# Value products of the samples as ScalarE copies, and the samples' loads issued from Pool's queue

## Chip, cores, metric

One core of one Trainium2 chip runs the whole kernel as one launch. The metric is the device time of one execution in microseconds; lower is better. The core has TensorE (PE in the profile), VectorE (DVE), ScalarE (ACT), GpSimd (POOL) and SyncE (SP). DMAs are issued by an engine's queue and moved by 16 DMA engines that all queues share.

## The reference, cut to what matters

The kernel computes one inference step of a two-layer decoder for a prompt of 1024 tokens and, sharing all weights, for 8 samples of one token each. Both layers have a mixer and a SwiGLU feed-forward part; both mixers hold a cross-attention over 256 memory tokens with 4 heads of 128, and layer 1 also holds a stick-breaking attention. For the samples the keys and values of these attentions are caches in HBM: `cache_mem_k` and `cache_mem_v` per layer and sample, and a paged pool `cache_sb_k`, `cache_sb_v`, of which each sample owns two pages of 128 tokens. So a sample's attention is one query row against 256 keys, and it shares no keys with the other samples.

```python
def mem_attend(q, mk, mv):
    s = jnp.einsum('blhd,bmhd->bhlm', q, mk) * (q.shape[-1] ** -0.5)
    p = jax.nn.softmax(s, axis=-1)
    return jnp.einsum('bhlm,bmhd->blhd', p, mv)

def stick_breaking(q, k, v, bias, q_pos, k_pos):   # per block of queries
    z = jnp.einsum('bqhd,bkhd->bhqk', qi, kf) * scale + bf
    log_keep = jnp.where(mask, jax.nn.log_sigmoid(-z), 0.0)
    tail = lax.cumsum(log_keep, axis=3, reverse=True) - log_keep
    w = jnp.where(mask, jnp.exp(jax.nn.log_sigmoid(z) + tail), 0.0)
    return jnp.einsum('bhqk,bkhd->bqhd', w, vf)
```

## The kernel before, in words

**Tiling.** The prompt is split in two groups of 512 tokens; group 1 also carries the 8 samples as 8 more columns (520). Activations stand with features on the 128 partitions. Every projection (`proj`, L256) is a product in three passes of float32r: weights and activations are split into a high and a low part, and high x high, high x low and low x high are added in PSUM. For it `split_w` (L240) loads weights of 4 x 128 rows by 128 columns from SyncE's queue (L245), casts them on ScalarE (L250) and subtracts on VectorE (L251). Raw weights have 5 buffers and split weights 5. Each projection of 1024 rows needs two such tiles; a down-projection in these parts one.

**Order of the work.** The code is a set of Python generators that are woven together by counts (`weave`), and the tile framework lays out each engine's own instruction sequence when the kernel is built; engines and queues then run in that sequence and wait on semaphores. The samples' work is in three streams, each woven with a part of a feed-forward network of the other group:

- `a1.mem_sample()` (layer 0, memory attention), with `f0.part(2)` and `f0.part(3)`;
- `b1.sb_sample()` (layer 1, stick-breaking over the pages), then
- `b1.mem_sample()` (layer 1, memory attention), both with `f0.part(2)` and `f0.part(3)` of layer 1.

A feed-forward part has gate and up projections first, with `silu` (L274: four ScalarE and two VectorE instructions) and the product L472 behind them, and then the down-projections, whose results VectorE adds up (L401).

**A sample stage.** `sample_scores` (L669) copies the queries (L672), transposes them on TensorE (L677), copies them to SBUF (L679) and writes them to a small HBM tile `qd` (L681). Then for each sample: load its keys, a tile `kt` of 128 partitions x 2 x 512 (512 KB); read its query row back from `qd`, repeated on all 128 partitions (`qb`, 256 KB, L687); multiply (L688); reduce each head's 128 columns (L689). `sample_pv` (L694) loads the sample's values `vt` in the same layout, multiplies each 128-column head block by the weight of that key and head (L700, one VectorE instruction over 128 x 1024), adds the two key halves (L701) and lets TensorE sum over the partitions with a selection matrix (L702), which puts each sample into its own row of one PSUM tile. `mem_loader` loads keys and values with one plain DMA (L717); `page_loader` gathers two pages with two indirect DMAs issued on Pool (L729).

**Buffers.** Key and value tiles come from `C()` (4 buffers of 128 x 1024 float32, also used for the memory's keys and values of the prompt and others), `qb` from `B()` (7 buffers), projections' PSUM from a pool of 2, other PSUM tiles from one of 3.

Of the kernel before, what the change touches and what calls it, by code (L numbers as in the profile page):

```python
# [12 lines left out]
AF = mybir.ActivationFunctionType  # L13
# [4 lines left out]
P = 128  # L18
# [4 lines left out]
def tile_decoder(  # L23
# [6 lines left out]
    nc = tc.nc  # L30
    D = x_prompt.shape[2]
    ND = D // P
    NB = x_sample.shape[0]
    NM = mem_prompt.shape[1]
    H = 4
# [32 lines left out]
    def nm(s):  # L68
        uid[0] += 1
        return f"{s}_{uid[0]}"  # L70
# [4 lines left out]
    def B(dt=F32):  # L75
        return bpool.tile([P, 512], dt, tag="b", name=nm("b"))
# [24 lines left out]
    def C():  # L101
        return cpool.tile([P, 2, 512], F32, tag="c", name=nm("c"))

    def S():
        return smp.tile([P, 512], F32, tag="s", name=nm("s"))

    def small(shape, dt=F32, tag="sm", bufs=None):
        return spool.tile(shape, dt, tag=tag, name=nm(tag), bufs=bufs)
# [39 lines left out]
    for lv in range(7):  # L148
# [3 lines left out]
        src = ones[:, 0:64].rearrange("p (b m) -> p b m", m=m)  # L152
        nc.gpsimd.affine_select(
            mf, src, pattern=[[-2 * m, nb], [0, m]], compare_op=ALU.is_ge, fill=0.0, base=0, channel_multiplier=1
# [115 lines left out]
    def split_to(dst, src):  # L270
        nc.scalar.copy(dst[0], src)  # L271
        nc.vector.tensor_sub(dst[1], src, dst[0].bitcast(F32))  # L272
# [396 lines left out]
    def sample_scores(q, load, sc):  # L669
        qc = small([P, H * NB], tag="ss")  # L670
        for i in range(2):
            nc.vector.tensor_copy(  # L672
                qc[:, i * 2 * NB : (i + 1) * 2 * NB].rearrange("p (h b) -> p h b", h=2), q[i][:, :, G : G + NB]
            )
        pq = S()
        for h in range(H):
            nc.tensor.transpose(pq[:NB, h * P : (h + 1) * P], qc[:, h * NB : (h + 1) * NB], ident)  # L677
        qt = B()
        nc.vector.tensor_copy(qt[:NB, :], pq[:NB, :])  # L679
        qd = tc.dram_tile([NB, 512], F32, name=nm("qd"))  # L680
        nc.sync.dma_start(qd, qt[:NB, :])  # L681
        yield
        scv = sc.rearrange("p (k h b) -> p k h b", k=2, h=H)
        for b in range(NB):
            kt = load(b)
            qb = B()
            nc.sync.dma_start(qb, qd[b].partition_broadcast(P))  # L687
            nc.vector.tensor_mul(kt, kt, qb.unsqueeze(1).to_broadcast([P, 2, 512]))  # L688
            nc.vector.tensor_reduce(  # L689
                scv[:, :, :, b], kt.rearrange("p k (h d) -> p k h d", h=H), axis=AX.X, op=ALU.add  # L690
            )
            yield

    def sample_pv(pT, load, xo, k0):  # L694
        po = S()
        pv4 = pT.rearrange("p (k h b) -> p k h b", k=2, h=H)
        for b in range(NB):
            vt = load(b)
            v4 = vt.rearrange("p k (h d) -> p k h d", h=H)
            nc.vector.tensor_mul(v4, v4, pv4[:, :, :, b].unsqueeze(3).to_broadcast([P, 2, H, P]))  # L700
            nc.vector.tensor_add(vt[:, 0, :], vt[:, 0, :], vt[:, 1, :])  # L701
            nc.tensor.matmul(po[:NB, :], sel[:, b, :], vt[:, 0, :], start=(b == 0), stop=(b == NB - 1))  # L702
            yield
        ot = B()
        nc.vector.tensor_copy(ot[:NB, :], po[:NB, :])
        pr = S()
        for h in range(H):
            nc.tensor.transpose(pr[:, h * NB : (h + 1) * NB], ot[:NB, h * P : (h + 1) * P], ident[:NB, :NB])
        for h in range(H):
            d = xo[k0 + h]  # L710
            split_to((d[:, 0, G : G + NB], d[:, 1, G : G + NB]), pr[:, h * NB : (h + 1) * NB])
        yield

    def mem_loader(src, l):
        def load(b):
            t = C()
            nc.sync.dma_start(t, src[l, b].rearrange("(k p) h d -> p k (h d)", p=P))  # L717
            return t

        return load  # L720
# [16 lines left out]
    def mem_attn_sample(l, qm, xo):  # L737
        HB = H * NB
        sc = small([P, 2 * HB], tag="sc", bufs=2)
        yield from sample_scores(qm, mem_loader(cache_mem_k, l), sc)  # L740
        pr = S()
        for blk in range(2):
            nc.tensor.transpose(pr[:HB, blk * P : (blk + 1) * P], sc[:, blk * HB : (blk + 1) * HB], ident)
        nmx = small([P, 2], tag="nmx")
        nc.vector.tensor_reduce(nmx[:HB, 0:1], pr[:HB, :NM], axis=AX.X, op=ALU.max, negate=True)
        sm = small([P, 2], tag="sme")
        pe = B()
        nc.scalar.activation(pe[:HB, :NM], pr[:HB, :NM], AF.Exp, bias=nmx[:HB, 0:1], accum_out=sm[:HB, 0:1])
        nc.vector.reciprocal(sm[:HB, 0:1], sm[:HB, 0:1])
        nc.vector.tensor_scalar(pe[:HB, :NM], pe[:HB, :NM], sm[:HB, 0:1], None, op0=ALU.mult)  # L750
        pb = S()
        for blk in range(2):
            nc.tensor.transpose(pb[:, blk * HB : (blk + 1) * HB], pe[:HB, blk * P : (blk + 1) * P], ident[:HB, :HB])
        pT = small([P, 2 * HB], tag="ss")
        nc.vector.tensor_copy(pT, pb[:, : 2 * HB])
        yield
        yield from sample_pv(pT, mem_loader(cache_mem_v, l), xo, H)
# [320 lines left out]
    def sb_sample(Qs, xo):  # L1078
        HB = H * NB
        zb = small([P, 2 * HB], tag="sc", bufs=2)  # L1080
        yield from sample_scores(Qs, page_loader(cache_sb_k), zb)
        nc.vector.tensor_add(zb, zb, biass.rearrange("p k h b -> p (k h b)"))
        e = small([P, 2 * HB], tag="ss")
        softplus_sp(zb, e, 2 * HB)
        cu = S()
        nc.tensor.matmul(cu[:, 0:HB], trif, e[:, 0:HB], start=True, stop=False)
        nc.tensor.matmul(cu[:, 0:HB], ones, e[:, HB : 2 * HB], start=False, stop=True)
        nc.tensor.matmul(cu[:, HB : 2 * HB], trif, e[:, HB : 2 * HB], start=True, stop=True)
        nc.vector.tensor_sub(zb, zb, cu[:, : 2 * HB])
        nc.scalar.activation(zb, zb, AF.Exp)  # L1090
        yield
        yield from sample_pv(zb, page_loader(cache_sb_v), xo, 0)
# [133 lines left out]
```

## Time and profile before

| what | value |
|---|---|
| runs shown | median 2563.17 us of 3 (2561.86 to 2564.59) |
| profiled execution | 2560.6 us, span 2558.9 us |
| TensorE, VectorE, ScalarE, GpSimd busy | 2525.4, 1556.9, 1218.0, 48.8 us |
| mean granted TensorE clock | 0.992 |
| SyncE's DMA queue | 454954 packets, 286.92 MB |
| issues concerned: L717, L687, L681 | 32 of 512 KB, 24 of 256 KB, 3 of 16 KB |
| median from issue to landing: L717, L687, L729 | 3.7, 6.1, 3.8 us |

How to read it: busy time of an engine is given with its share of the span and the number of instructions. Line rows name the line, the engine, the operation and the tiles written and read, then how often, the busy time and mean duration, and the idle time of that engine just before with what ended it. In a timeline the columns are start, duration, engine, line, operation, tiles and count, then in brackets the idle time before and its releaser. Matmuls overlap, so a single one's duration is longer than its share of the engine's time.

### The profile page before, as it was taken

The numbers are of one execution on the slowest core, as the hardware profiler recorded it, in microseconds if no ns is written. First come the engines' busy times: TensorE is split into PE (matmuls) and PEld (weight loads), VectorE is DVE, ScalarE is ACT, GpSimd is POOL, SyncE is SP. The second block draws the span as 40 slices with busy tenths as digits, with TensorE's granted clock in tenths as the row PEclk, the third lists the DMA queues.
The fourth block names the chain that finished last, engine by engine and source line by source line (L and its number), as shares of the span: only waits on it lengthen the run. The fifth ranks groups of instructions, "written<-read, shape, count | busy, mean of one in ns | idle before, by whom it ended". The sixth has DMA issues, their size and how long they took to land.

```text
span 2558.9 us, 40442 instructions
## 1 busy us (share of the span) xinstructions
PE 2525.4 (99%) x15649; PEld 2203.6 (86%) x15649; DVE 1556.9 (61%) x2709; ACT 1218.0 (48%) x2290; POOL 48.8 (2%) x59
## 2 busy tenths in 40 slices
PE   8999999999999999999999999999999999999998
PEld 6888898888777888999999989767776798999998
DVE  6666466654765577555544577666677758444445
ACT  6346543343434445555433455566543245443334
POOL 1000000000000000000000000000041000000000
PEclk9999999999999999999999999999999999999999
DMA  6352242233642445322333445322156444333332
GB/s 186 111 158 71 74 149 81 60 111 112 202 144 87 128 154 178 105 81 63 99 92 93 127 151 180 111 87 67 53 180 211 148 125 124 110 88 101 94 92 68
DMA packets 457707, 297.90 MB, mean 116 GB/s; under 512 B 17573, under 2 KB 422642, under 8 KB 457514
## 3 DMA queue, kind: packets, MB, share of 16 engines
q1 hardware_dynamic: 454954, 286.92, 37.2%
q0 software_dynamic: 2560, 8.39, 1.1%
q8 instruction: 123, 2.02, 0.3%
q14 instruction: 70, 0.57, 0.1%
HBM read 265.44 MB, written 29.80 MB: 115 GB/s over the span
## 4 chain that ended last, share of the span: by engine, by line
issue 25%; PE 23%; DVE 1%; POOL 1%; DMA 0%; ACT 0%; DVEq 0%; POOLq 0%
PE mm L264 22%; POOL c L729 1%; PE s L702 0%; DMA c<-in_cache_sb_k,pidx 0%; DVE ws L251 0%; DVE sc L689 0%; DMA b<-qd 0%; DVE t L280 0%; DMA c<-in_cache_sb_v,pidx 0%; PE s L1123 0%; PE ns L291 0%; PE s L438 0%; DVE yT L540 0%; DVE t L283 0%; DVE c L688 0%
## 5 line engine op out<-in xcount | busy, mean ns | idle before, releaser
L264 PE MATMUL mm<-x,ws 128*128 128x260 f32 (+1 forms) x10080 | 1676.2, 324 | 10.7 <-DVE ws L251 4.2
L264 PEld LDWEIGHTS mm<-x,ws 128*128 128x128 f32 x10080 | 1451.1, 189 | 171.7 <-issue 21.5
L251 DVE TENSOR_TENSOR ws<-w,ws 128x512 fp32r<-128x512 f32 (+1 forms) x800 | 522.5, 657 | 533.5 <-ACT ws L250 522.6
L250 ACT CAST ws<-w 128x512 fp32r<-128x512 f32 (+1 forms) x800 | 474.3, 593 | 694.0 <-PE mm L264 624.1
L264 PE MATMUL mm<-m,ws 128*128 128x260 f32 (+1 forms) x3168 | 543.2, 326 | 1.1 <-DVE r L401 0.6
L264 PEld LDWEIGHTS mm<-m,ws 128*128 128x128 f32 x3168 | 453.8, 188 | 59.9 <-issue 15.0
L277 ACT ACTIVATE t<-mm 128x512 f32<-128x512 f32 (+1 forms) x104 | 62.5, 601 | 195.8 <-PE mm L264 195.7
L401 DVE TENSOR_TENSOR r<-r,mm 128x520 f32<-128x520 f32 (+1 forms) x128 | 88.3, 690 | 97.6 <-PE mm L264 96.5
L472 DVE TENSOR_TENSOR t<-t,mm 128x512 f32<-128x512 f32 (+1 forms) x88 | 60.8, 691 | 72.2 <-PE mm L264 72.1
L280 DVE SCALAR_TENSOR_TENSOR t<-mm,t 128x512 f32<-128x512 f32 (+1 forms) x104 | 72.1, 693 | 43.6 <-ACT t L279 43.4
L281 ACT ACTIVATE t<-t 128x512 f32<-128x512 f32 (+1 forms) x104 | 65.9, 634 | 11.8 <-DVE t L280 11.7
L302 DVE TENSOR_TENSOR st<-st,n 128x512 f32<-128x512 f32 (+1 forms) x98 | 67.0, 690 | 6.5 <-ACT n L301 4.6
L279 ACT ACTIVATE t<-t 128x512 f32<-128x512 f32 (+1 forms) x104 | 66.0, 635 | 2.8
L278 ACT ACTIVATE t<-t 128x512 f32<-128x512 f32 (+1 forms) x104 | 66.2, 637 | 0.0
L283 DVE TENSOR_TENSOR t<-t,mm 128x512 f32<-128x512 f32 (+1 forms) x88 | 60.3, 685 | 5.4 <-ACT t L281 4.8
L271 ACT CAST m<-t 128x512 fp32r<-128x512 f32 (+1 forms) x88 | 54.9, 623 | 18.0 <-DVE t L472 11.3
L272 DVE TENSOR_TENSOR m<-t,m 128x512 fp32r<-128x512 f32 (+1 forms) x88 | 61.0, 693 | 3.9 <-ACT m L271 1.9
L729 POOL DMA_INDIRECT c<-in_cache_sb_k,pidx x16 | 22.7, 1416 | 1869.9 <-DVE r L401 1244.1
L890 PEld LDWEIGHTS s<-a,a 128*128 128x128 f32 x448 | 53.4, 192 | 1.2
L890 PE MATMUL s<-a,a 128*128 128x64 f32 x448 | 53.2, 271 | 0.0
L1025 DVE SCALAR_TENSOR_TENSOR b<-b,b 128x512 f32<-128x512 f32 (+3 forms) x48 | 26.8, 558 | 30.6 <-ACT b L1024 30.1
L641 ACT ACTIVATE b<-s,nmx 128x256 f32<-128x256 f32 x64 | 29.7, 469 | 28.2 <-DVE nmx L635 28.2
(291 smaller groups left out, 1960.9 us busy)
## 6 DMA issues: line engine op xcount, KB each, us to landing
w<-in_w_gu SPq DMA_DIRECT2D x352, 256.0 KB, 2.9
w<-in_w_down SPq DMA_DIRECT2D x160, 256.0 KB, 2.7
w<-in_w_in_a SPq DMA_DIRECT2D x80, 256.0 KB, 3.0
w<-in_w_o SPq DMA_DIRECT2D x64, 256.0 KB, 2.8
w<-in_w_mem_kv SPq DMA_DIRECT2D x32, 256.0 KB, 3.0
c<-in_cache_mem_k SPq DMA_DIRECT2D x16, 512.0 KB, 3.7
c<-in_cache_mem_v SPq DMA_DIRECT2D x16, 512.0 KB, 3.7
w<-in_w_kv SPq DMA_DIRECT2D x32, 256.0 KB, 3.0
```

Of the source, the lines that this page charges most:

```text
L250: nc.scalar.copy(ws[:, 0, :n, :], raw[:, :n, :])
L251: nc.vector.tensor_sub(ws[:, 1, :n, :], raw[:, :n, :], ws[:, 0, :n, :].bitcast(F32))
L264: nc.tensor.matmul(ps[:, a, : PW[g]], wt, xt[k][:, xi, o : o + PW[g]], start=(k == 0 and wi == 0), stop=(k == nk - 1 and wi == 2),)
L272: nc.vector.tensor_sub(dst[1], src, dst[0].bitcast(F32))
L277: nc.scalar.activation(av, pv(ps, g), AF.Abs)
L278: nc.scalar.activation(av, av, AF.Exp, scale=-1.0)
L279: nc.scalar.activation(av, av, AF.Ln, bias=1.0)
L280: nc.vector.scalar_tensor_tensor(av, pv(ps, g), 0.0, av, op0=ALU.min, op1=ALU.subtract)
L281: nc.scalar.activation(av, av, AF.Exp)
L302: nc.vector.tensor_add(acc[:, :n], acc[:, :n], t[:, :n])
L401: nc.vector.tensor_add(dst, dst, pv(ps, g))
L890: nc.tensor.matmul(plv[:, hh, c, :], K_[:, hh, cs], rhs, start=True, stop=True)
```

## The change

Two things are edited. In `sample_pv` the one VectorE product per sample becomes eight ScalarE copies, one for each key half and head, each over 128 columns and scaled by the weight column of that half, head and sample; the add of the two halves stays on VectorE and the sum on TensorE. And three kinds of DMA of the sample stages are issued by Pool in place of SyncE: the write of the queries to `qd`, the broadcast reads of `qd`, and the plain loads of memory keys and values. The page gathers were on Pool already.

```diff
@@ sample_scores
         qd = tc.dram_tile([NB, 512], F32, name=nm("qd"))
-        nc.sync.dma_start(qd, qt[:NB, :])
+        nc.gpsimd.dma_start(qd, qt[:NB, :])
...
             kt = load(b)
             qb = B()
-            nc.sync.dma_start(qb, qd[b].partition_broadcast(P))
+            nc.gpsimd.dma_start(qb, qd[b].partition_broadcast(P))
@@ sample_pv
             v4 = vt.rearrange("p k (h d) -> p k h d", h=H)
-            nc.vector.tensor_mul(v4, v4, pv4[:, :, :, b].unsqueeze(3).to_broadcast([P, 2, H, P]))
+            for k in range(2):
+                for h in range(H):
+                    nc.scalar.activation(v4[:, k, h, :], v4[:, k, h, :], AF.Copy, scale=pv4[:, k, h, b : b + 1])
@@ mem_loader
             t = C()
-            nc.sync.dma_start(t, src[l, b].rearrange("(k p) h d -> p k (h d)", p=P))
+            nc.gpsimd.dma_start(t, src[l, b].rearrange("(k p) h d -> p k (h d)", p=P))
```

## The prediction

> **What bounds the kernel now.** I read the page first, for the share of each engine, then the windows by stage around the three sample stages, then the timeline of the worst of them, and last the lines that the change touches.
>
> ```profile
> PE 2525.4 (99%) x15649; PEld 2203.6 (86%) x15649; DVE 1556.9 (61%) x2709; ACT 1218.0 (48%) x2290; POOL 48.8 (2%) x59
> ...
> q0 software_dynamic: 2560, 8.39, 1.1%
> ```
>
> TensorE is busy for 99% of the span, so only its idle stretches and its clock can move. The samples' work stands in three stages: about 647 to 767 us (layer 0, memory attention), 1875 to 1956 (layer 1, stick-breaking over the pages), 1957 to 2034 (layer 1, memory attention). Each has a score part (L688, L689) and a value part (L700 to L702). The windows by stage, in order: score and value of the pages, score and value of layer 1's memory, score and value of layer 0's memory (columns: stretch, its length, then busy time and count of PE, PEld, DVE, ACT, POOL, the granted clock, DMA share, GB/s):
>
> ```profile
> 1885.50:1902.50 17.00, 12.91 (x52) 9.70 (x51) 16.94 (x20) 5.48 (x10) 11.41 (x8) 0.90 0.76 244
> 1926.50:1948.80 22.30, 21.46 (x80) 12.59 (x79) 19.13 (x25) 3.10 (x5) 8.90 (x8) 1.00 0.55 166
> 1963.50:1984.00 20.50, 17.06 (x73) 13.18 (x71) 20.40 (x24) 9.38 (x16) 0.00 (x0) 1.00 0.76 241
> 2011.40:2031.30 19.90, 19.90 (x71) 10.66 (x70) 18.63 (x24) 2.49 (x4) 0.00 (x0) 1.00 0.39 129
> 655.00:684.00 29.00, 27.58 (x120) 22.15 (x119) 28.72 (x35) 12.66 (x21) 0.00 (x0) 1.00 0.90 277
> 721.00:748.00 27.00, 27.00 (x107) 18.33 (x108) 22.81 (x31) 8.79 (x15) 0.00 (x0) 1.00 0.58 175
> ```
>
> In the score parts VectorE has no free time (16.94 of 17.00, 20.40 of 20.50, 28.72 of 29.00) and TensorE idles 4.09, 3.44 and 1.42 us. In the value parts VectorE is busy too, but TensorE idles only 0.84 us in the first and nothing in the others. The timeline of the pages' score part shows how:
>
> ```profile
> 1885.56 1.23 DVE L688 TENSOR_TENSOR c<-c,b 128x1024 f32<-128x1024 f32 x1 [0.63 <-DMA b<-qd]
> ...
> 1899.88 2.49 DVE L251 TENSOR_TENSOR ws<-w,ws 128x512 fp32r<-128x512 f32 x4
> 1899.95 5.50 POOL L729 DMA_INDIRECT c<-in_cache_sb_k,pidx x1 [0.30 <-issue]
> 1900.62 12.30 PEld L264 LDWEIGHTS mm<-x,ws 128*128 128x128 f32 x44 [3.10 <-DVE ws L251]
> 1900.62 23.83 PE L264 MATMUL mm<-x,ws 128*128 128x512 f32 x92 [2.67 <-DVE ws L251]
> ```
>
> The weight splits (L251) queue behind score products, and TensorE waits for them. The wait costs twice: an undisturbed pair of projections, x48, takes 11.05 us (at 655.88), 0.230 each, so 92 would take 21.2 and took 23.83, at a granted clock of 0.71 in 1900 to 1910. After the idle time at 1984 the next 44 took 11.88 in place of 10.1. So 7.5 us of idle time in these two places brought 4.4 us at a low clock: 0.58 us for each us idle.
>
> **The change, part by part.** The rows that price it:
>
> ```profile
> L688 DVE TENSOR_TENSOR c<-c,b x24: 1211/1218/1258, 654.9 to 1986.8; 128x1024 f32<-128x1024 f32 x24
> ...
> L701 DVE TENSOR_TENSOR c<-c x24: 677/683/686, 723.3 to 2028.1; 128x512 f32<-128x512 f32 x24
> ...
> L250 ACT CAST ws<-w 128x128 fp32r<-128x128 f32 x64 | 19.0, 297 | 88.8 <-PE mm L264 81.8 <-issue 5.3 <-ACT b L641 1.5
> ...
> L353 ACT ACTIVATE x<-ns,par 128x512 fp32r<-128x512 f32 x8 | 5.6, 695 | 2.5 <-PE ns L350 2.5
> ```
>
> **Removed from VectorE:** 24 products of L700 at 1.22 us, 29.2 us, all in the value parts. The only TensorE time there to gain is the idle 0.84 us; the score parts' VectorE work (24 x (1.218 + 1.212) = 58.3 us) is untouched. Gain 0.8, bounds 0 and 0.8.
>
> **Added to ScalarE:** 8 copies of 128x128 for each of 24 samples, 192 in all, 64 in each value part. A plain 128x128 cast takes 0.297; a copy with a scale per partition takes 0.695 at 128x512 (L353), and an element costs (0.619 - 0.297)/384 = 0.84 ns between the two sizes of L250, so 0.695 - 0.322 = 0.373 at 128x128. Independent neighbours start closer than they last (L277 at 600.61 lasts 0.60, the next starts 0.49 later). From start to start I bound it by 0.28 and 0.40 and take 0.31, nearer the overlapped row since the eight touch different columns. 64 x 0.31 = 19.8 us. With what ScalarE already does in the three value parts (3.10, 2.49, 8.79) this makes 22.9 in 22.3, 22.3 in 19.9, 28.6 in 27.0: over by 0.6, 2.4 and 1.6, sum 4.6. At 0.28 the sum is 0.5, at 0.40 it is 22. ScalarE thus becomes the engine of the value part. Queued behind the copies there are its weight casts (L250), for which L251 and then TensorE wait; their cover is five split buffers, each half a gate projection, 5 x 2.76 = 14 us of matmuls. The samples' own matmul (L702) stands in TensorE's order with down-projections around it, and 20 of these (4.9 us) still follow the last one at 2033.71. I charge half: 2.3 us, bounds 0 and 22.
> By the Trainium skill (ScalarE: Activation LUTs, What ACT_TABLE_LOAD costs) an activation takes 186 ns and 0.833 ns per element, 93 more for a pointer operand, and neighbours overlap by 93. That gives an estimate of 386 ns lasting and 293 from start to start, so 18.8 us a part and an overrun of 2.0 in place of 4.6; the row's 373 agrees with the first figure, and no row here shows the second.
>
> **Moved from SyncE's queue to Pool's:** 32 loads of memory K and V, 24 query broadcasts, 3 writes of the queries, 59 in all. Their bytes are the same. Buffers set the loads' times: SyncE issued the fifth K load at 660.27, as the first reduction ended, so on Pool they go no earlier. SyncE is rid of 59 issues of 0.3 to 0.46 us and of their waits, but no weight came late for these: it stood still from 1887 to 1900.6 because the splits that free weight buffers were late. I count 0, with 1 us either way.
> The price of a plain load on Pool is not in the trace. Near rows are the gathers: 0.945 us plus 0.30 to the next in quiet time, 1.25, and 8 of them from 1888.79 to 1905.45, 2.08 each, beside a full VectorE (one lasted 5.50). Below, 0.30 as on SyncE. I take 1.25. What is late then is the start of each score part: write, then first broadcast, in sequence. In the third stage the write was issued at 1958.05, the first broadcast at 1959.53, and VectorE, after waiting 2.02 us, began at 1963.51. Two dearer issues add 2 x 0.95 - 0.30 - 0.43, about 1.2, and a gap of 0.3: 1.5 us; at 2.08 each 3.4. In the page stage Pool also has gathers at 1880.35 and 1881.60, just when the query write is wanted (1879.26): 1.5 if the write stands ahead of them, 4.8 behind; I take 3. Sum 1.5 + 1.5 + 3 = 6.0, bounds 0 and 12. VectorE is full right behind each start, so this is backlog for the splits; the buffers ahead soften it. I take 0.6, 3.6 us of TensorE idle time, and 0.58 of that for the clock, 2.1.
>
> **Sum:** -0.8 + 2.3 + 0 + 3.6 + 2.1 = +7.2 us. The profiled execution took 2560.6 us (span 2558.9), 2.6 below the median 2563.2; carried to the median 2570.
>
> **The rivals.**
> **Faster.** The score part's cost is a burst: eight products and reductions ahead of four splits. Broadcasts that arrive one per Pool issue, not seven within 3.8 us as at 1881.27, could let splits pass between them. At stake are 4.09 + 3.44 + 1.42 idle and 4.4 of clock, 13.4 us; half of it gives 2556. For it: the burst is plain in the rows. Against it: VectorE's demand stays. An x48 step of TensorE (11.05) carries 5.4 us of splits and gate work and 2.5 samples at 2.43, 11.5 in all, and an in-order VectorE that waits for a broadcast lets no split pass.
> **Pool feeds too slowly.** If every issue costs the 2.08 us of the full stretch, the eight broadcasts that join the page gathers put its last score up to 16.6 us later. Half of it lost, with its clock, is 8.3 x 1.58 = 13 on top of 7: 2583. For it: the gather of 5.50 us ran while VectorE had two-input work back to back. Against it: a plain load reads no index, and VectorE, once it waits, leaves Pool alone.
> The Trainium skill (SBUF — State Buffer, SBUF: two separate sides) says that VectorE and GpSimd share a port pair, and that descriptors for a DMA issued on Pool can't be written while VectorE holds it, so such loads are better issued from SP. The 5.50 us fits; no run here shows a plain load under it.
> **ScalarE copies at 0.40 us:** overrun 22, half exposed, with clock 17, and 5.7 of late starts: 2586. For it: eight small instructions for one. Against it: the overlap seen in L277.
> **Everything hidden:** later starts are absorbed by the ready splits and ScalarE keeps pace: 2563.
>
> **How the numbers follow.** Forecast 0.43, own range 2563 to 2580; hidden 0.20; faster 0.15; Pool 0.12; ScalarE 0.10. I call within 0.2% (5.1 us) no change, about what a measurement here can tell. Slower: the last two and four fifths of the forecast, 0.57, and a little of the hidden case, 0.59; faster 0.15; the rest, 0.26, is no change. From 2556 to 2588 leaves out the tails of the faster and the ScalarE case.
>
> **What would show it.** Right: VectorE's first L688 of each stage 1.5 to 5 us later against its query copy (L679); ScalarE near 9 tenths in the value parts, its copies 0.3 us apart; TensorE's idle time in the score parts up by some 4 us, waiting for L251, with a clock dip behind it. Wrong: Pool issues at SyncE's price, or TensorE idle less in the score parts (then the faster rival); TensorE waiting at L702 for ScalarE by more than 3 us a part (then the ScalarE rival); VectorE waiting for key loads in mid-part (then Pool).

## The result, and the profile after

The changed kernel took 2566.64 us (median of 22 runs, 2563.1 to 2573.12), the kernel before 2561.7 us on the same chip (22 runs, 2554.05 to 2564.88). The ratio is 1.0025, with a 95% interval from 1.0018 to 1.0032: slower by 4.9 us between the medians and by 6.4 by the ratio, which is not that of the medians; +7.2 was forecast. The profiled execution of the changed kernel has a span of 2565.3 us, 6.4 more than before's, at a mean granted clock of 0.991.

The edit shifts the line numbers: the copies are L702, the add of the halves L703, the sample's matmul L704, the plain loads L719, the page gathers L731.

The page of the kernel after, busy time of each engine, then the queue that Pool feeds (packets, MB, share):

```profile
PE 2527.6 (99%) x15649; PEld 2202.8 (86%) x15649; DVE 1530.4 (60%) x2685; ACT 1273.0 (50%) x2482; POOL 85.1 (3%) x118
...
q0 software_dynamic: 9184, 31.51, 3.8%
```

VectorE works 26.5 us less, ScalarE 55.0 more, GpSimd 36.3 more, and TensorE still works for all but some 38 us of the span. So the few lost microseconds are in short places. The windows by stage of the kernel after, in the order of the prediction's table (score and value of the pages, of layer 1's memory, of layer 0's memory):

```profile
1887.00:1904.00 17.00, 11.35 (x44) 8.32 (x43) 16.44 (x19) 5.27 (x9) 11.52 (x9) 0.87 0.64 223
1927.00:1950.00 23.00, 23.00 (x83) 13.11 (x82) 9.82 (x16) 20.36 (x68) 9.64 (x10) 1.00 0.52 156
1965.00:1998.50 33.50, 27.37 (x107) 21.46 (x107) 28.74 (x34) 12.22 (x22) 7.54 (x12) 0.90 0.67 211
2015.00:2038.50 23.50, 22.58 (x77) 11.31 (x75) 10.10 (x17) 21.92 (x70) 2.86 (x4) 1.00 0.34 104
655.00:684.00 29.00, 27.72 (x121) 22.23 (x120) 28.57 (x35) 12.65 (x21) 5.62 (x8) 1.00 0.86 274
721.00:748.00 27.00, 27.00 (x106) 17.86 (x106) 13.13 (x21) 24.79 (x74) 2.90 (x4) 1.00 0.50 161
```

Read the idle time of TensorE as length less busy time. In the value part of layer 1's memory ScalarE is now all but full (21.92 of 23.50) and VectorE has time to spare (10.10); the same holds for layer 0's (24.79 of 27.00). Layer 0's stage loses next to nothing: TensorE idles 1.28 us in its score part, 1.42 before, and none in its value part, as before. In the third row TensorE idles 6.13 us.

The totals of two single profiles don't locate a loss of 5 us. Some low-clock time between 514 and 644 us, ahead of all samples' work, differs between the profiles of kernels that are alike there, and moved single spans by -6 to +1.7 us. So the start of the n-th projection matmul (L264) was compared between the two traces, n by n: TensorE runs the projections in the same order in all kernels, and the growth of the difference within a stage is what that stage lost. For the kernel after, in us of before's time:

```
15-514   514-644   644-804   804-1672   1672-1954   1954-2004   2004-2041   2041-2540   all
 +0.0      -0.0      +0.2      -0.3       +0.7        +3.5        +1.9        +0.0      +6.3
                  layer 0's memory         pages     score part  value part
                                                     of layer 1's memory
```

Nearly all of it, 5.4 of 6.3 us, is in the last of the three stages. Its start in the kernel after (columns: start, duration, engine, line, operation, tiles and count, then idle time before it and its releaser):

```profile
1939.85 2.45 ACT L702 ACTIVATE c<-c,sc 128x128 f32<-128x128 f32 x8 [0.69 <-DMA c<-in_cache_sb_v,pidx]
...
1949.55 2.68 ACT L250 CAST ws<-w 128x512 fp32r<-128x512 f32 x5
...
1958.22 0.68 DVE L679 COPY b<-s 8x512 f32<-8x512 f32 x1 [0.18 <-PE s L677]
...
1959.20 0.56 POOL L681 DMA_DIRECT2D qd<-b  x1 [6.62 <-DVE b L679]
...
1962.54 3.76 POOL L687 DMA_DIRECT2D b<-qd  x7 [2.78 <-DMA qd<-b]
...
1967.04 2.36 DVE L688 TENSOR_TENSOR c<-c,b 128x1024 f32<-128x1024 f32 x2 [4.69 <-DMA b<-qd]
...
1972.90 14.05 PE L264 MATMUL mm<-x,ws 128*128 128x512 f32 x50 [3.83 <-DVE t L283]
```

and the same place in the kernel before:

```profile
1957.34 0.68 DVE L679 COPY b<-s 8x512 f32<-8x512 f32 x1 [0.19 <-PE s L677]
...
1958.05 0.30 SPq L681 DMA_DIRECT2D qd<-b  x1
...
1959.53 3.30 SPq L687 DMA_DIRECT2D b<-qd  x6
...
1963.51 2.36 DVE L688 TENSOR_TENSOR c<-c,b 128x1024 f32<-128x1024 f32 x2 [2.02 <-DMA b<-qd]
...
1969.38 11.62 PE L264 MATMUL mm<-x,ws 128*128 128x512 f32 x50 [1.15 <-DVE t L283]
```

Count from the query copy (L679). Before: write after 0.71, first broadcast after 2.19, first score product after 6.17 us. After: 0.98, 4.32, 8.82. The product is 2.65 us later, VectorE stands idle for 4.69 in place of 2.02, everything behind it on VectorE is late, and TensorE waits 3.83 in place of 1.15 us for a gate's last product (L283). The next 50 matmuls then take 14.05 in place of 11.62 us. In windows of 6 us the granted clock is 0.94 from 1966, 0.50 from 1972 and 0.99 from 1978 in the kernel after, which makes 6.8 us at half speed; before it is 0.72 from 1984 and full around it, 3.4 us at half speed. So the part pays 2.7 us of idle time and up to 1.7 of clock, and comes out 3.5 later. The wait that grew is the one for the gate's last product; TensorE's other two in this part, for L472 (0.77 us) and for a weight split (L251, 1.53 and 1.54), are as long as before.

Two more things are to be seen. Most of the lateness lies between write and first broadcast, that is, in the landing of 16 KB in HBM (from issue to issue 1.48 us before, 3.34 after). And ahead of it ScalarE runs five weight casts in a row at 1949.55, behind the copies; before, they stand apart, at 1946.10, 1948.88, 1953.68, 1956.47 and 1960.15. The last copies themselves wait for page values, 2.6 us in three waits, and the casts stand behind them in ScalarE's sequence. What the casts do to the DMAs is seen in windows (stretch, length, busy time and count of PE, PEld, DVE, ACT, POOL, clock, DMA share, GB/s), first before:

```profile
1950.00:1953.00 3.00, 3.00 (x12) 1.99 (x11) 1.92 (x4) 0.00 (x0) 0.00 (x0) 1.00 0.86 228
...
1956.00:1959.00 3.00, 3.00 (x19) 2.21 (x18) 2.12 (x5) 1.01 (x4) 0.00 (x0) 1.00 0.47 148
1959.00:1962.00 3.00, 3.00 (x15) 2.49 (x14) 1.02 (x3) 0.79 (x2) 0.00 (x0) 1.00 0.59 165
```

then after:

```profile
1950.00:1953.00 3.00, 3.00 (x11) 1.42 (x10) 3.00 (x6) 2.23 (x5) 1.43 (x2) 1.00 0.27 86
...
1956.00:1959.00 3.00, 3.00 (x19) 2.25 (x18) 1.37 (x2) 0.40 (x1) 0.00 (x0) 1.00 1.13 328
1959.00:1962.00 3.00, 3.00 (x15) 2.49 (x14) 1.53 (x6) 1.41 (x6) 0.56 (x1) 1.00 0.98 232
```

Raw weight buffers come free when they have been cast and split. Held back and then cast in one go, they let the next weights go out in a lump: the DMA share is 0.27 while the buffers are held and 1.13 and 0.98 just when the queries are written and read back, where before it was 0.47 and 0.59.

### The profile page after: what moved, and what is told of

The parts are those of the page before. It is cut to its first block, busy times and chain, and to the rows that moved or that the text cites. A ratio compares the mean times of both kernels' runs of the same rounds, so it can differ in the third digit from the quotient of the medians.

```text
span 2565.3 us, 40650 instructions
## 1 busy us (share of the span) xinstructions
PE 2527.6 (99%) x15649; PEld 2202.8 (86%) x15649; DVE 1530.4 (60%) x2685; ACT 1273.0 (50%) x2482; POOL 85.1 (3%) x118
## 3 DMA queue, kind: packets, MB, share of 16 engines
q8 instruction: 123, 2.02, 0.3%
## 4 chain that ended last, share of the span: by engine, by line
PE 54%; DVE 3%; ACT 1%; issue 1%; DMA 1%; POOL 0%; DVEq 0%; ACTq 0%; SPq 0%; POOLq 0%
PE mm L264 47%; PE s L1063 1%; PE s L1075 1%; PE s L1048 1%; PE s L661 1%; PE s L704 1%; PE s L630 1%; DVE ws L251 0%; DMA b<-qd 0%; PE s L654 0%; PE ns L291 0%; DVE sc L689 0%; DVE c L688 0%; DVE st L302 0%; PE s L1004 0%
## 5 line engine op out<-in xcount | busy, mean ns | idle before, releaser
L264 PE MATMUL mm<-x,ws 128*128 128x260 f32 (+1 forms) x10080 | 1676.7, 324 | 14.2 <-DVE t L283 7.7
L264 PEld LDWEIGHTS mm<-x,ws 128*128 128x128 f32 x10080 | 1451.4, 189 | 176.7 <-issue 23.6
L251 DVE TENSOR_TENSOR ws<-w,ws 128x512 fp32r<-128x512 f32 (+1 forms) x800 | 522.8, 658 | 532.3 <-ACT ws L250 527.3
L264 PE MATMUL mm<-m,ws 128*128 128x260 f32 (+1 forms) x3168 | 544.4, 326 | 1.1 <-DVE r L401 0.6
L264 PEld LDWEIGHTS mm<-m,ws 128*128 128x128 f32 x3168 | 453.4, 188 | 62.9 <-issue 17.5
L472 DVE TENSOR_TENSOR t<-t,mm 128x512 f32<-128x512 f32 (+1 forms) x88 | 60.8, 691 | 71.4 <-PE mm L264 71.2
L283 DVE TENSOR_TENSOR t<-t,mm 128x512 f32<-128x512 f32 (+1 forms) x88 | 60.3, 686 | 5.5 <-ACT t L281 4.8
L731 POOL DMA_INDIRECT c<-in_cache_sb_k,pidx x16 | 22.2, 1387 | 1134.9 <-PE s L630 1127.3
```

Source lines behind the costliest of these rows:

```text
L251: nc.vector.tensor_sub(ws[:, 1, :n, :], raw[:, :n, :], ws[:, 0, :n, :].bitcast(F32))
L264: nc.tensor.matmul(ps[:, a, : PW[g]], wt, xt[k][:, xi, o : o + PW[g]], start=(k == 0 and wi == 0), stop=(k == nk - 1 and wi == 2),)
```

## The experiments

All were timed in five rounds against the kernel before on the same chip; a ratio is to that kernel, with its 95% interval, and a cost in us is worked out from the ratio. The first question was which edit costs: the copies, the queries' two DMAs, the keys and values, or only some of them together. The rivals of the late start were that the copies alone cost all, and that Pool feeds the keys and values too slowly.

### The copies alone

```diff
 (against the change: all loads back on SyncE)
-        nc.gpsimd.dma_start(qd, qt[:NB, :])
+        nc.sync.dma_start(qd, qt[:NB, :])
...
-            nc.gpsimd.dma_start(qb, qd[b].partition_broadcast(P))
+            nc.sync.dma_start(qb, qd[b].partition_broadcast(P))
...
-            nc.gpsimd.dma_start(t, src[l, b].rearrange("(k p) h d -> p k (h d)", p=P))
+            nc.sync.dma_start(t, src[l, b].rearrange("(k p) h d -> p k (h d)", p=P))
```

> Only the ScalarE copies; all sample loads stay on SyncE. Theory A (the loss is the late query broadcast of the last sample stage, 2.7 us of TensorE idle time and 1.7 us of clock, and the copies cost about 1.9 us in the last value part and give back what they gain in the others): +0.5 to +2.0 us against before, with the third stage's first L688 again about 3 us ahead of where the changed kernel has it. Rival B (the copies are the loss): +4 to +6 us. Rival C (the key and value loads on Pool are the loss): 0 to +2 us as in A.

Measured: 2562.41 us, 1.0004 [0.9992, 1.0017]. No difference can be told from this time. By segments the value part of layer 1's memory loses 1.9 us, as in the change, and its score part 0.4.

### The loads alone

```diff
 (against the change: the product back on VectorE)
-            for k in range(2):
-                for h in range(H):
-                    nc.scalar.activation(v4[:, k, h, :], v4[:, k, h, :], AF.Copy, scale=pv4[:, k, h, b : b + 1])
+            nc.vector.tensor_mul(v4, v4, pv4[:, :, :, b].unsqueeze(3).to_broadcast([P, 2, H, P]))
```

> All three kinds of DMA on Pool, the value products back on VectorE in one instruction. Theory A: +3 to +4.5 us against before, from the third stage's start. Rival B: 0 within 1 us. Rival C: +3 to +5 us.

Measured: 2562.02 us, 0.9998 [0.9989, 1.0008]. No difference, where theory A had said +3 to +4.5 us. So neither edit costs by itself what both cost together, and neither rival in which one edit alone costs all is left. Their sum, +0.02%, is below the change's +0.25%; at the upper ends of the intervals (0.17 + 0.08) they would reach it, so the two runs leave an additive cost possible, and the next ones were to tell.

### The queries alone, and the keys and values alone

```diff
 (against the kernel before; first kernel)
-        nc.sync.dma_start(qd, qt[:NB, :])
+        nc.gpsimd.dma_start(qd, qt[:NB, :])
...
-            nc.sync.dma_start(qb, qd[b].partition_broadcast(P))
+            nc.gpsimd.dma_start(qb, qd[b].partition_broadcast(P))
```

> Only the write of the queries and their broadcasts on Pool; key and value loads on SyncE, value products on VectorE. Theory A: +3 to +4.5 us, the same as with all loads moved. Rival B: 0 within 1 us. Rival C: 0 within 1 us.

```diff
 (against the kernel before; second kernel)
-            nc.sync.dma_start(t, src[l, b].rearrange("(k p) h d -> p k (h d)", p=P))
+            nc.gpsimd.dma_start(t, src[l, b].rearrange("(k p) h d -> p k (h d)", p=P))
```

> Only the plain key and value loads on Pool; queries on SyncE, value products on VectorE. Theory A: 0 within 1 us. Rival B: 0 within 1 us. Rival C: +3 to +5 us.

Measured: queries 2563.28 us, 1.0004 [0.9995, 1.0013]; keys and values 2561.64 us, 0.9993 [0.9984, 1.0002]. Neither is a cost that can be told from none, and theory A missed again with the queries. On the prices, the rows of the kernel after (ns least, median, most):

```profile
L681 POOL DMA_DIRECT2D qd<-b x3: 558/562/565, 648.2 to 1959.2; - x3
```

```profile
L687 POOL DMA_DIRECT2D b<-qd x24: 539/539/599, 650.3 to 1968.6; - x24
```

```profile
L719 POOL DMA_DIRECT2D c<-in_cache_mem_k x16: 711/724/942, 583.2 to 1981.7; - x16
```

A plain issue takes Pool 0.54 to 0.72 us, about 0.25 more than SyncE, and the longest of all took 0.94. No issue took longer than that, though VectorE was full in the score parts; two of the page gathers in the same trace did:

```profile
1899.23 2.42 POOL L731 DMA_INDIRECT c<-in_cache_sb_k,pidx  x1 [0.33 <-issue]
1901.96 5.50 POOL L731 DMA_INDIRECT c<-in_cache_sb_k,pidx  x1 [0.31 <-issue]
```

The loads landed later, though: from issue to landing the page has a median of 5.8 us for memory keys and 4.8 for memory values, where before it was 3.7 for both. The engines hardly felt it: VectorE waited for no memory key, and ScalarE 0.8 us in all for memory values.

### The change with one kind of load back on SyncE

```diff
 (against the change; first kernel: the queries' write and broadcasts)
-        nc.gpsimd.dma_start(qd, qt[:NB, :])
+        nc.sync.dma_start(qd, qt[:NB, :])
...
-            nc.gpsimd.dma_start(qb, qd[b].partition_broadcast(P))
+            nc.sync.dma_start(qb, qd[b].partition_broadcast(P))
```

> The change with the query write and the broadcasts back on SyncE; copies on ScalarE, key and value loads on Pool. Engine sequences are those of the changed kernel. Theory D (an interaction: the copies hold back weight casts, so weight loads go out in a lump after the page value part; with the queries on Pool the lump runs beside the query write and broadcasts and makes them late, with the queries on SyncE the later weights stand behind them in one queue): +0 to +2 us against before. Theory E (no interaction: copies about +2.5, queries on Pool about +2, key and value loads nothing): +2 to +3 us.

```diff
 (against the change; second kernel: the keys and values)
-            nc.gpsimd.dma_start(t, src[l, b].rearrange("(k p) h d -> p k (h d)", p=P))
+            nc.sync.dma_start(t, src[l, b].rearrange("(k p) h d -> p k (h d)", p=P))
```

> The change with only the key and value loads back on SyncE; copies on ScalarE, queries on Pool. Theory D: SyncE's queue again holds key loads that break up the weight lump, but the queries stand apart from the weights: +3 to +5 us, the third stage's first L688 8 us or more behind its query copy. Theory E: +4 to +5 us. A third reading, in which the key loads on Pool are what collides with the queries: +0 to +2 us.

Measured: copies with keys and values 2563.6 us, 1.0009 [0.9998, 1.002]; copies with queries 2568.08 us, 1.0033 [1.0021, 1.0046]. The first, +2.3 us, lies between the two theories and decides nothing. The second, +8.4 us, is above what either theory said; its interval overlaps the change's and lies above those of the copies alone and of the queries alone, so it takes the copies and the queries to have the whole cost. No effect of the keys' and values' queue is seen.

### Which stage's copies

The copies of the pages' stage precede the stage that loses. So one kernel takes those back to VectorE, and one keeps only those.

```diff
 (against the change; in the second kernel the condition is k0 == H)
+            if k0 == 0:
+                nc.vector.tensor_mul(v4, v4, pv4[:, :, :, b].unsqueeze(3).to_broadcast([P, 2, H, P]))
+            else:
                 for k in range(2):
                     for h in range(H):
                         nc.scalar.activation(v4[:, k, h, :], v4[:, k, h, :], AF.Copy, scale=pv4[:, k, h, b : b + 1])
```

> The change, but the page stage's value products are one VectorE instruction per sample as before; the two memory stages keep the ScalarE copies, all loads stay on Pool. Theory D: without copies ahead of the third stage no lump; the first L688 of that stage about 7 us behind its query copy, and +0 to +3 us left from the last value part. Theory E: two thirds of the copies' cost and all of the queries', +3 to +4 us.

> All loads on Pool, ScalarE copies in the page stage only; the two memory stages keep the VectorE product. Theory D: the lump and the late third stage are there: +3 to +5 us. Theory E: a third of the copies' cost and all of the queries', +2 to +3 us.

Measured: pages on VectorE 2564.19 us, 1.0016 [1.0005, 1.0027]; only the pages copied 2563.69 us, 1.0016 [1.0004, 1.0029]. The times don't part them: by its time (+4.1 us) the first is above theory D's range, and the second, also +4.1, within it. The segments do. With the pages on VectorE the third stage's score part loses 0.1 us and its value part 1.9; with only the pages copied the score part loses 3.7 and the value part nothing. The casts of the latter show the same row of five:

```profile
1946.93 2.68 ACT L250 CAST ws<-w 128x512 fp32r<-128x512 f32 x5
```

So the value part's loss comes from its own copies, and most of the score part's goes with the copies of the stage before; of what it consists is seen below. The first kernel's +0.16% (4 us) is more than the 1.9 us found in it; its lower end is 1.3 us, and the rest stays open.

Over the kernels so far the third stage's start sorts as follows (us after its query copy; then for the score part's segment in that one profile the loss, TensorE's idle time and the time at half clock):

```
                              page    queries  first      first            TensorE  half
                              copies  on       broadcast  product   loss   idle     clock
before                          no    SyncE      2.19       6.17      -     3.4      3.4
keys and values alone           no    SyncE      2.19       6.78    +2.9    4.9      6.8
loads alone                     no    Pool       3.07       7.04    -0.7    4.3      0
queries alone                   no    Pool       3.69       7.48    +1.9    5.3      3.4
change, pages on VectorE        no    Pool       3.07       6.77    +0.1    5.1      0
copies alone                    yes   SyncE      3.38       6.68    +0.4    4.0      3.4
copies with keys and values     yes   SyncE      3.61       7.86    +3.0    5.3      6.8
copies with queries             yes   Pool       4.67       8.91    +3.6    6.3      6.8
only pages copied               yes   Pool       4.47       8.69    +3.7    6.0      6.8
the change                      yes   Pool       4.32       8.82    +3.5    6.1      6.8
```

The first broadcast is 0.9 to 1.5 us late with the queries on Pool, 1.2 to 1.4 with page copies, and 2.1 to 2.5 with both: the lateness adds up. The lump goes with the page copies in all of them: in the 3 us behind the query copy the DMA share is 1.04 to 1.13 in the five kernels with page copies and 0.21 to 0.44 in the five without. From the write to the first broadcast pass 1.5 us on SyncE's queue and 2.1 to 2.7 on Pool's without the lump, 2.7 to 2.9 and 3.3 to 3.7 with it.

TensorE's idle time nearly adds up too. It grows by 0.9 to 1.8 us with the queries on Pool, by 0.6 to 1.9 with page copies, and by 2.6 to 2.8 with both: each edit alone does seem to cost idle time there, too little to be told from these times. (The keys and values alone, with neither, have 1.5 more.) The time at half clock does not follow it closely. All three kernels with both have 6.8 us of it, the others 0, 3.4 or 6.8 (none with 5.1 us of idle time, 6.8 with 4.9), and it sets much of the loss: the keys and values alone, with a start of 6.78, lose 2.9 us by 1.5 more idle and 3.4 more at half clock, while the loads alone gain by having none. So the loss in one profile is uncertain by some 1.7 to 3.4 us, and the idle time is the steadier measure. That the two edits cost more together than the sum of each alone is therefore likely from the times (0.04% and 0.04% against 0.25% and 0.33%) and not certain.

### Half of the copies

A version that could beat both kernels: ScalarE copies only the second key half, VectorE multiplies the first, so that neither fills the value part. It was run with all loads on Pool and with all on SyncE.

```diff
 (against the change; the second kernel has all loads on SyncE besides)
-            for k in range(2):
-                for h in range(H):
-                    nc.scalar.activation(v4[:, k, h, :], v4[:, k, h, :], AF.Copy, scale=pv4[:, k, h, b : b + 1])
+            for h in range(H):
+                nc.scalar.activation(v4[:, 1, h, :], v4[:, 1, h, :], AF.Copy, scale=pv4[:, 1, h, b : b + 1])
+            nc.vector.tensor_mul(v4[:, 0], v4[:, 0], pv4[:, 0, :, b].unsqueeze(2).to_broadcast([P, H, P]))
```

> All loads on Pool as in the change, but only one key half of each sample's product is copied on ScalarE (4 copies, about 1.2 us); VectorE multiplies the other half. Theory D: with half the copies ScalarE keeps pace with its casts, so no five casts in a row at the end of the page value part, the third stage's first L688 about 7 us behind its query copy, and the last value part no longer 1.9 us longer: 0 to +1.5 us against before. Rival E (each copy costs its share): +2 to +3 us.

> As the one before with all sample loads on SyncE. Theory D: -1 to +1 us against before. Rival E: +1 to +2 us.

Measured: on Pool 2563.9 us, 1.0013 [1.0003, 1.0022]; on SyncE 2562.19 us, 1.0001 [0.9992, 1.001]. On Pool the third stage starts after 6.94 us, with the first broadcast after 3.07 as in the kernels without page copies, and its score part loses nothing (-0.8, with no time at half clock). Its value part still loses 1.9 us, with 1.4 of waiting for adds, and the time of +3.3 us is above theory D's 0 to +1.5: here theory D missed. On SyncE the time is within its range (+0.3 us), and the value part loses 0.6; in its one profile, though, the third stage's first product comes after 7.95 us with the first broadcast at 2.19, and the score part loses 1.8. That is a late start without a lump, and why the broadcasts landed late is open. Both lose 2.8 us in the pages' stage, with 10.2 us at half clock where before has 6.8. Neither beats the kernel before.

### Half of the score product on GpSimd

In the score parts VectorE is full, so this takes 128 x 512 of each score product off it; everything else is the kernel before.

```diff
 (against the kernel before)
-            nc.vector.tensor_mul(kt, kt, qb.unsqueeze(1).to_broadcast([P, 2, 512]))
+            nc.gpsimd.tensor_mul(kt[:, 1, :], kt[:, 1, :], qb)
+            nc.vector.tensor_mul(kt[:, 0, :], kt[:, 0, :], qb)
```

> The kernel before with one key half of each score product on GpSimd, value products on VectorE, loads on SyncE. If the score parts are bound by VectorE alone, 24 x 0.6 us less there shortens its demand in a projection step from 11.5 to about 10 us against TensorE's 11.05: -3 to -8 us. If GpSimd and VectorE hold each other up on a shared port, VectorE's two-input work gets longer: 0 to +5 us.

Measured: 2566.79 us, 1.0019 [1.0008, 1.003]: the hoped-for gain did not come, and +4.9 us lies in the range of the other branch. The two halves in its trace:

```profile
L688 POOL TENSOR_TENSOR c<-c,b x24: 1262/1380/1805, 655.7 to 1992.1; 128x512 f32<-128x512 f32 x24
```

```profile
L689 DVE TENSOR_TENSOR c<-c,b x24: 675/688/2173, 655.6 to 1998.0; 128x512 f32<-128x512 f32 x24
```

GpSimd needs twice VectorE's time for the same half, and some of VectorE's products last 2.17 in place of 0.69 us beside it: all seven over 1.1 us overlap one of GpSimd's. Layer 0's stage is 5.7 us later by its segment, with 3.0 us more idle time and 6.8 us at half clock where before has none.

### The queries of the last stage written early

If the late start costs the 3.5 us, and not something else in the copies, it must go when the start doesn't wait for the write. Here the queries of layer 1's memory attention are transposed and written at the start of the pages' stage; the copies, the queues and the order of the rest are the change's.

```diff
 (against the change)
+        def query(self):
+            yield from sample_query(self.Qm, self.got)
...
-    weave((chain(b1.sb_sample(), b1.mem_sample()), 40), (chain(f0.part(2), f0.part(3)), 16))
+    weave((chain(b1.query(), b1.sb_sample(), b1.mem_sample()), 40), (chain(f0.part(2), f0.part(3)), 16))
```

> The change, with the queries of layer 1's memory attention transposed and written to HBM at the start of the page stage, some 75 us before they are read. All copies stay on ScalarE and all loads on Pool, so the lump of weight casts and loads at the end of the page value part stays. Theory D: the third stage's first L688 no longer waits for the write and the broadcasts, and most of the 3.5 us that the score part lost comes back; the 1.9 us of the last value part stay: +0 to +2.5 us against before. If the lump or the copies cost the time in another way than through the late queries: +4 to +6 us, as the change.

Measured: 2563.31 us, 1.0011 [1.0, 1.0022]. Its third stage (L693 is the broadcast and L694 the product here):

```profile
1959.11 3.77 POOL L693 DMA_DIRECT2D b<-qd  x7
...
1965.25 2.36 DVE L694 TENSOR_TENSOR c<-c,b 128x1024 f32<-128x1024 f32 x2 [2.21 <-DMA b<-qd]
...
1972.26 11.63 PE L264 MATMUL mm<-x,ws 128*128 128x512 f32 x50 [2.48 <-DVE t L283]
```

VectorE waits 2.21 us for the first broadcast, as before the change (2.02), and the 50 matmuls behind take 11.63 at full clock. TensorE's idle time in the score part falls from 6.1 to 3.3 us, as before the change (3.4), and the segment goes from +3.5 to -1.1 us; that it is below zero is the clock, with none of it at half where before has 3.4 us. The value part's segment stays at +1.9. The lump of weights is still there (DMA shares of 1.02 and 1.27 in 1956 to 1962), so in this stage it costs by way of the queries. The whole time, +2.8 us, is just above theory D's range and below the rival's, and its interval overlaps the change's (from 1.0018 on), so for the whole kernel the gain is likely and not certain; for the stage the trace shows it.

### The value part's 1.9 us

TensorE's own timeline through the third value part, first rows to last, before:

```profile
2010.26 4.90 PE L264 MATMUL mm<-m,ws 128*128 128x512 f32 x20
2015.09 1.88 PE L702 MATMUL s<-c,sel 128*8 128x512 f32 x4
2016.90 2.81 PE L264 MATMUL mm<-m,ws 128*128 128x512 f32 x11
```

and after:

```profile
2020.23 1.65 PE L264 MATMUL mm<-m,ws 128*128 128x512 f32 x6
2021.81 1.02 PE L704 MATMUL s<-c,sel 128*8 128x512 f32 x2
2022.76 1.90 PE L264 MATMUL mm<-m,ws 128*128 128x512 f32 x7
...
2036.16 0.96 PE L264 MATMUL mm<-m,ws 128*128 128x512 f32 x3
2038.04 1.02 PE L704 MATMUL s<-c,sel 128*8 128x512 f32 x2 [0.92 <-DVE c L703]
```

0.92 us is a wait for the last sample's add, which waits for ScalarE. The rest has no idle time. From start to start a run of 20 projection matmuls takes 4.83 us and one of 6 takes 1.58, so 0.232 each and 0.19 a run; four sample matmuls take 1.81 and two 0.955, so 0.43 each and 0.10 a visit. Before, the eight samples came in 5 visits, three of them with two samples; after, each comes alone, 8 visits. Three more cost 3 x 0.29 = 0.87, with 0.92 some 1.8 of the 1.9 us. That the visits cost it is worked out from these rows; no run varied them alone. Other parts agree: layer 0's value part has six visits with the copies and five before, no idle time in either, and takes 55.42 us for the same projections in place of 55.09; the half copies on SyncE have six in the third value part and lose 0.57 us, 0.21 of it idle.

## Why the prediction was right

**Sign, size and chief term.** Slower was forecast by 7.2 us, by way of late score parts and the clock behind them; 4.9 was measured (6.4 by the ratio), and the score part's late start is the largest piece of it, 3.5 us with its clock. The experiment with the early queries bears out that path. In these two parts of the sum, 3.6 us of idle time and 2.1 of clock, the changed kernel shows 3.4 more idle in the pages' stage and the last score part and 3.4 more at half clock, which is 1.7. What made the start late, and where, was another thing than the prediction had.

**ScalarE's copies, +2.3.** Right in pitch, near in size in part by luck, wrong in the wait. From start to start a copy takes 0.295 us where 0.31 was taken. The value parts of the kernel after:

```profile
2015.40 14.29 ACT L702 ACTIVATE c<-c,ss 128x128 f32<-128x128 f32 x48 [0.23 <-DVE ss L757]
```

```profile
L702 ACT ACTIVATE c<-c,ss x128: 384/387/403, 721.7 to 2034.6; 128x128 f32<-128x128 f32 x128
```

48 in a row take 14.29 us, and (14.29 - 0.39)/47 = 0.295. The Trainium skill (ScalarE: Activation LUTs, What ACT_TABLE_LOAD costs) gives by its figures, as an estimate, 386 ns lasting and 293 from start to start; both agree with these rows within 3 ns. A loss came in the last value part alone, 1.9 us, where 2.4 of the 4.6 had been put; the two others hid theirs. The wait that was charged, weight splits held up behind late casts, came in no value part: in the last one TensorE waited 0.92 us for a sample's add, and some 0.9 went to its three extra visits, for which the prediction has no term. The casts that the copies did hold back told in the next stage. TensorE's wait at the sample's matmul stayed below the 3 us that would have spoken for the rival of slow copies.

**VectorE freed, -0.8.** The idle 0.84 us in the pages' value part is gone (23.00 of 23.00), and for the same projections that part takes 29.68 us in place of 30.12: six visits of the samples in place of four take back the rest. Ahead of it the stage's score part lost 0.9, so the stage as a whole came out 0.7 later.

**SyncE's queue, 0 with 1 either way.** The keys and values alone came out at -0.07%, -1.8 us with an interval from -4.1 to +0.5, which can't be told from 0.

**The late start, +3.6 and +2.1.** The size was near, by errors that offset each other. The step "I take 1.25" for an issue on Pool was wrong: 0.54 to 0.72, near SyncE's price, which the prediction had named as a mark against itself. So of the "Sum 1.5 + 1.5 + 3 = 6.0" the parts came out at -0.4 in layer 0's stage (7.60 us after the query copy, 7.98 before), +1.7 in the pages' and +2.65 in the last, 4.0 in all; the pages' late start cost 0.9 us, the last one 3.5 with its clock. The backlog was to show as waits for weight splits (L251). Even before the change these were only 4.2 of the 7.5 us, and after it 4.0: the waits that grew are those for the gate's last product (L283), from 1.5 to 5.9 us. By the queue alone (the loads alone) the last would have been 0.9 later. What the step lacked is in none of its terms: the copies of the stage before bunch the weight casts, the casts bunch the weight loads, and the queries' write has to land beside them. The two edits were priced one by one, and neither price holds the lateness that they have together.

That the lump delays the write is read from the DMA shares and from the first broadcasts, some 1.2 us later with page copies whichever queue carries them; no run varied the lump alone. The Trainium skill (DMA: Bandwidth & Descriptors, Queues, rings and completion order) says that each DMA engine takes turns among the queues that have work for it, which would let weights of SyncE's queue run between the packets of Pool's; no run here shows the turns themselves.

**The rivals.** "Faster" fell: late broadcasts let no split pass, TensorE idled longer. "Pool feeds too slowly" fell: no issue of a plain load took longer than 0.94 us, and ScalarE waited 0.8 us in all for memory loads. Gathers did take longer in a score part, 2.42 and 5.50 us; why they and not the plain loads, no run here shows. "ScalarE copies at 0.40 us" fell with the 0.295 from start to start. "Everything hidden" describes each edit alone by its time, and not both.

## What to carry to other kernels

Two edits whose cost can't be told from none can cost together when they make the same thing late: here each made the first read back at the start of a stage 0.9 to 1.5 us late and TensorE 0.6 to 1.9 us more idle, and the two together 2.1 to 2.5 late and 2.6 to 2.8 more idle, with a stretch at half clock behind it. When work is moved to an engine that also prepares weights, look at what its delayed work releases next: here buffers that came free together sent their loads out together. The small transfer that a stage waits for should be issued well ahead of that moment. Moving work off an engine gains only in those parts in which that engine ends last: here the products left VectorE where it held up next to nothing, 0.84 us in one of three parts.

## What was not expected of the hardware

- A plain DMA costs Pool 0.54 us an issue (seven broadcasts in 3.76 us) and 0.72 for a 512 KB load, also beside a full VectorE, where a gather on the same queue went from 0.95 to 5.50 us.
- The time at half clock came in lumps of about 3.4 us: 3.4 before and 6.8 after in the third stage, the first behind 2.30 us of idle time, the second from within the 3.83 us. The same 2.30 us of idle time drew a lump in the kernel before and none in the kernel after (1984 to 1996, clock 1.00). And from 514 to 644 us, with some 0.65 us of idle time in all in every kernel, 6.8 to 23.9 us ran at half clock. The Trainium skill (TensorE: Matmul & The Clock Gate, What's actually happening) describes a free-running window of 3.4 us, with which the lengths of the lumps agree (3.4, 6.8 and 10.2 us).
- A change of TensorE between projection and sample matmuls costs about 0.29 us there and back by the working above, without any idle time in the profile (0.33 for one visit more in layer 0's value part).
- A product on GpSimd (1.38 us for 128 x 512) goes with a VectorE product beside it of up to 2.17 in place of 0.69 us.
